# Nineteen weight slots for the experts, filled in the order of reading, and first weights loaded by rows

## The chip, the cores and the metric

The program runs on one core of a Trainium2 chip. A core has TensorE (PE, matmuls and transposes), VectorE (DVE), ScalarE (ACT), GpSimd (POOL), and SyncE (SP), which here only issues DMAs. ACT and POOL issue DMAs too; the transfers of all queues run on the same 16 DMA engines. The metric is device time in microseconds, lower is better. The kernel before takes 425.59 us, the median of three runs (425.16 to 427.43).

## The reference

One inference step of a decoder layer, for 256 prompt tokens and 32 sample tokens (8 sequences of 4), width 1024, float32:

```
h = RMSNorm(x) @ w_in                       # 1024 x 5120: q, k, v of two branches, two gates
A = stick-breaking attention (8 heads x 64); B = MoBA attention (8 heads x 64)   # sample tokens: paged caches
x = x + (sigmoid(g_A) * (A @ w_proj_sb) + sigmoid(g_B) * (B @ w_proj_moba)) @ w_out
t = RMSNorm(x)
group = top 1 of 4; experts = top 2 of the group's 4; weights w from the softmaxes
x = x + sum over the two experts of w * (silu(t @ w_gate[e]) * (t @ w_up[e])) @ w_down[e]
y = RMSNorm(x) * g_final
```

The outputs are y and the new keys and values of both branches. The 16 experts have three matrices of 1 MB each: 48 MB of weights, all read.

## The kernel before, in words

**Order.** PE's order is the order of the code. Two streams are woven by hand by `Driver` (L78): dense work, and latency-bound work that is spawned with an estimated delay. In the startup, in the routing and in the end ACT and DVE are held to the order of the code as well (`manual_schedule`); elsewhere, and on SP and POOL throughout, a scheduler with a simulated timeline orders the instructions and chooses the storage of each tile when it becomes free. A DMA on SP waits in SP's order for its storage to be free, and for the landing of an earlier DMA whose semaphore it reuses.

**Startup (L201 to L304).** x arrives in three blocks of rows (two of the prompt, one of the sample) and is turned into columns by PE (L247, six groups: three blocks by two halves of the width). DVE multiplies the turned blocks by g_mix (`mul`, L232; g_mix itself is turned by PE at L251), ACT rounds the product to a high part (`high`, L236), DVE or POOL takes the low rest (`low`, L240). The first weights, 256 columns of w_in (`raw("i2")`, L317), come in two column halves of 128 columns each. ACT rounds the first half to `h` (L263), DVE subtracts for `l` (L270), and PE multiplies high by high, high by low and low by high parts (L276), the upper rows of the weights first. The second half (`h5`, `l5`, L277) goes through `held` (L347 to L351). `square(t)` gives the sum of squares of a block on ACT; the reciprocal root reaches PE as a diagonal matrix, whose product with ones is the row `rb` (L297). Constants (a table, of which the identity comes first, and the page table) are issued on ACT's queue, L160 and L161.

**Middle.** The rest of the projection, attention, the merge, w_out. PE's order runs through without a pause of note.

**Experts (L817 to the end).** Experts are taken in pairs, pr = 0 to 7. Tokens are sorted to 64 places per expert, so that one block of 128 rows serves a pair. `up(pr)` multiplies the gathered rows, in eight steps k, by the gate and up weights of both experts; `down(pr, h)` runs a while later, in the middle of `up(pr + 1)`, after its step 3. A part of the weights is a triple (pair, kind, expert of the pair): kind 0 is the gate and up weights of steps 0 to 3, kind 1 those of steps 4 to 7, kind 2 is w_down; each is 1 MB, 8 KB per partition. `parts` (L819) lists the 48 parts in the order (pr, 0), (pr, 1), (pr, 2). `ring_slot(n)` takes the n-th slot of a ring made of four pools of 8, 5, 3 and 2 slots (`RINGS`, L75), 18 in all. The first 18 parts are loaded as the pools come to be (L850 to L900, the last ones around the store of x2, `rows_out`); `ring_loads(30)` (L1159) writes the other 30, each of which waits for a slot to be read. `xes` are three buffers for rows: one is filled by PE for pair 0 (`pick`, L980), the other two by gathers for the pairs after it (`fetch`, L970).

**End.** The results of pairs 0 to 5 go to DRAM as they come (`y_d`, L1203), and `gathered()` (L1232) brings each token its two rows back by six gathers from POOL's queue (L1239) into three slots of the ring, which DVE adds to x2 (L1246). Pairs 6 and 7 are added by matmuls with a selection matrix (`combine`, L1249). DVE's written order has the adds of the gathered rows ahead of pair 7's `h` (L1164). `final_out` multiplies by g_final (`gfb`, read into xes[0] at L1143) and stores y.

Of the kernel before, what the change touches and what calls it, by code (L numbers as in the profile page):

```python
# [7 lines left out]
F32 = mybir.dt.float32  # L8
# [4 lines left out]
ALU = mybir.AluOpType  # L13
# [4 lines left out]
D = 1024  # L18
NP_, NS = 256, 32
NT = NP_ + NS  # L20
# [53 lines left out]

RINGS = (8, 5, 3, 2)  # L75

# [45 lines left out]
def build(tc, I, O):  # L122
    nc = tc.nc
# [35 lines left out]
    nc.sync.dma_start(xs[2][0:32], I["x_sample"])  # L159
    nc.scalar.dma_start(ptb, I["page_table"][None, :].broadcast_to([128, 16]))  # L160
    nc.scalar.dma_start(blob[:, 128:], I["blob"][:, 128:])  # L161

    def cc(name):
# [37 lines left out]
    def startup():  # L201

        hold = tc.manual_schedule(engines={mybir.EngineType.Activation, mybir.EngineType.DVE})
        hold.__enter__()
        r = raw("i2", w_in[:, :, 512:768])
        dg = [at.tile([128, 128], F32, tag="t2", name=f"dg{t}", bufs=5) for t in range(3)]
        junk = at.tile([128, D], F32, tag="pg", name="junk", bufs=5)
# [33 lines left out]

        warm(2, 416)
        for i in range(6):
            ks, cols, n = place(i)
            pv = P(("at", "at", "at", "at", "ss", "po")[i], f"xt{i}")[:, 0:4 * n].rearrange("p (k t) -> p k t", k=4)
            for k in range(4):
                nc.tensor.transpose(pv[:, k, :], xsrc[i % 3][:, (ks.start + k) * 128:(ks.start + k + 1) * 128], ident[:n, :n])  # L247
            pvs.append(pv)
            if i == 0:
                pg = P("mm", "gm")  # L250
                nc.tensor.transpose(pg[:, 0:8], g8, ident[0:8, 0:8])  # L251
                V.tensor_copy(gmix, pg[:, 0:8])
        square(0)
        square(1)
        for i in range(4):
# [6 lines left out]
        h = wp.tile([128, 8, 128], F32R, tag="wh", name="hi4")  # L262
        nc.scalar.copy(h, r[:, :, 0:128])  # L263
        mul(4)
# [12 lines left out]
        h5 = split_h(r[:, :, 128:256], "i5")  # L277
        l5 = split_l(r[:, :, 128:256], h5, "i5")
        square(2)
        keep_raw(0)  # L280
# [10 lines left out]
        second = held(h5, l5, ks_of(xTh, 8), ks_of(xTl, 8), o5)  # L291
        for _ in range(6):
            next(second)
# [18 lines left out]
    def raw(key, src, shape=(8, 256)):  # L312
        if key not in raws:
            t = wr.tile([128, *shape], F32, tag="raw", name=f"raw{key}")
            if key == "i2":
                for hf in range(2):
                    nc.sync.dma_start(t[:, :, hf * 128:(hf + 1) * 128], src[:, :, hf * 128:(hf + 1) * 128])  # L317
            else:
                load = nc.sync.dma_start(t, src)
                if key in ring_after:  # L320
                    with tc.issue_after(load.ins):
                        ring_loads(ring_after[key])
            raws[key] = t
        return raws[key]
# [493 lines left out]
    W = {}  # L818
    parts = [(pr, kind, i) for pr in range(8) for kind in (0, 1, 2) for i in range(2)]  # L819

# [58 lines left out]
    V.memset(lg, 0.0)  # L879
    xes = [wk.tile([128, D + 4], F32, name=f"xe{i}") for i in range(3)]  # L880
    for i in range(3):
        nc.gpsimd.memset(xes[(i + 1) % 3], 0.0)
    nc.gpsimd.dma_start(y_d[NONE:, :], xes[0][0:16, 0:D])
# [85 lines left out]
    def fetch(pr):  # L969
        return nc.gpsimd.indirect_dma_start(out=xes[1 + pr % 2], out_offset=None, in_=x2_d[:, :],  # L970
                                            in_offset=bass.IndirectOffsetOnAxis(ap=inv[:, pr:pr + 1], axis=0),
                                            bounds_check=NT - 1, oob_is_err=False)


    def pick(c):
        po = P("at", f"xe0{c}")
        cs = slice(c * 512, c * 512 + 512)
        for t in range(3):
            mm(po, slots_of(t, 0), x2[:TW[t], t, cs], start=(t == 0), stop=(t == 2))
        (nc.scalar.copy, V.tensor_copy)[c](xes[0][:, cs], po)  # L980

# [36 lines left out]
    for t in range(3):  # L1018
        mm(pi[:, 16:17], slots_of(t, 0), x2[:TW[t], t, D:D + 1], start=(t == 0), stop=(t == 2))
    pick(0)  # L1020
    index_mm(0, 3)
# [6 lines left out]
    V.tensor_copy(rsl[0], pi[:, 16:17])  # L1028
    turn_xe(xeTs[0], xes[0], 0)
    V.tensor_reduce(es, ee, axis=AX.X, op=ALU.add)  # L1030
# [50 lines left out]
    def overflow():  # L1081
        cnt = nc.values_load(mxi[0:1, 0:1], min_val=0, max_val=NT)
        xnT = [mo.tile([128, 4, 128], F32, tag="yl", name=f"oxn{i}", bufs=2) for i in range(2)]
        wt = xes[2][:, 0:512].rearrange("p (k f) -> p k f", k=4)
        wdt = xes[2][:, 512:1024]
        hh = mo.tile([128, 256], F32, tag="h", name="ohh")
        hT = mo.tile([128, 256], F32, tag="hT", name="ohT")
        cwe = mo.tile([128, 2], F32, name="cwe")
        with tc.If(cnt > CAP):
            for t in range(3):  # L1090
                n = TW[t]
                r = x2[:n, t, D:D + 1]
                nc.scalar.dma_start(xes[1][:n], x2_d[t * 128:t * 128 + n, :])
                for k in range(8):
                    pt = P("at", f"ox{t}{k}")
                    nc.tensor.transpose(pt[:, 0:n], xes[1][:n, k:D:8], ident[:n, :n])
                    V.tensor_scalar_mul(xnT[k // 4][:, k % 4, 0:n], pt[:, 0:n], gpk[:, k:k + 1])
# [30 lines left out]

    gfb = xes[0][:, 0:D]
    fz = xes[1][:, 0:D]  # L1130

    def turn(pr):
        xeT = gt.tile([128, 4 * NT], F32, tag="xT", name=f"xeT{pr}")[:, 0:D].rearrange("p (k t) -> p k t", k=8)
        rsl[pr] = mo.tile([128, 1], F32, tag="rsl", name=f"rsl{pr}", bufs=3)
        i = turn_xe(xeT, xes[1 + pr % 2], pr)
        with tc.issue_after(i.ins):
            V.tensor_copy(rsl[pr], xes[1 + pr % 2][:, D:D + 1])  # L1137
        xeTs[pr] = xeT

    def up(pr):  # L1140
        pt = P("mm", f"gu{pr}")
        if pr == 6:
            nc.sync.dma_start(gfb, I["g_final"][None, :].broadcast_to([128, D]))  # L1143
        for k in range(8):
# [24 lines left out]
    def down(pr, h):  # L1169
# [16 lines left out]
        if LATE <= pr < 7:  # L1186
            y = mo.tile([128, D], F32, tag="y", name=f"y{pr}")
        for c in range(2):
# [85 lines left out]
    def final_square(t, c):  # L1274
        n = TW[t]
        junk = gt.tile([128, 4 * NT], F32, tag="xT", name=f"fj{t}{c}")[:, 0:512]
        nc.scalar.activation(junk[:n], x2[:n, t, c * 512:(c + 1) * 512], AF.Square, accum_out=st[:n, t, c:c + 1])
        if t == 1:
            nc.gpsimd.tensor_tensor(fz[:, c * 512:(c + 1) * 512], x2[:, t, c * 512:(c + 1) * 512], gfb[:, c * 512:(c + 1) * 512], op=ALU.mult)
        if c:  # L1280
            V.tensor_scalar(st[:n, t, 2:3], st[:n, t, 0:1], 1.0 / D, EPS, op0=ALU.mult, op1=ALU.add)
            nc.scalar.activation(st[:n, t, 3:4], st[:n, t, 1:2], AF.Ln, bias=st[:n, t, 2:3], scale=1.0 / D)
            nc.scalar.activation(st[:n, t, 3:4], st[:n, t, 3:4], AF.Exp, scale=-0.5)
# [3 lines left out]
    def final_out(t):  # L1287
# [5 lines left out]
        for u in range(2 if t < 2 else 1):  # L1293
            us = slice(u * 512, (u + 1) * 512) if t < 2 else slice(0, D)
            if t == 1:
                V.tensor_scalar_mul(fz[:, us], fz[:, us], st[:n, t, 3:4])
                nc.sync.dma_start(out[:, us], fz[:, us])
                continue
            V.scalar_tensor_tensor(y[:, us], x2[:n, t, us], st[:n, t, 3:4], gfb[:n, us], op0=ALU.mult, op1=ALU.mult)
            nc.sync.dma_start(out[:, us], y[:, us])  # L1300
# [52 lines left out]
```

## Time and profile before

| | |
|---|---|
| median of three runs | 425.59 us |
| profiled execution, its own time | 427.94 us |
| its span, first to last instruction | 426.2 us |
| PE busy | 396.5 us (93%) |
| DVE, ACT, POOL busy | 201.7, 177.5, 97.2 us |
| mean granted TensorE clock | 0.971 of full speed |
| moved by DMA | 111.65 MB, mean 262 GB/s |
| of the chain that ended last | PE 69%, DMA 21%, DVE 4% |

Rows of the order of instructions give the start in us from the span's start, the duration in us, engine, line, operation, the tile written and those read, and in brackets the engine's idle time before and what ended it; SPq is a DMA issue on SP. Rows of merged instructions carry a count. The stage table adds the granted clock and the mean busy share of the 16 DMA engines, with their rate.

### The profile page before, as it was taken

Reading aid. Unit: us, or ns where it says so; the run is one execution under the profiler, and the core shown is the slowest. Engines: PE = TensorE matmul, PEld = TensorE weight load, DVE = VectorE, ACT = ScalarE, POOL = GpSimd, SP = SyncE. Lnnn points to the kernel's source line nnn. Section 1 sums busy time; section 2 is a strip of 40 time slices with the busy share of each in tenths; the row PEclk is TensorE's granted clock in tenths of the full one; section 3 lists DMA queues with packets and bytes.
Section 4 is the critical chain, followed back from the end, with each engine's and each line's share of the span. In section 5 each row is a group of like instructions: output and inputs, shape, how many; then the busy total and the mean of one; then the engine's idle time right before and its main releaser. Section 6 shows DMA issues by size and latency. Waiting matters only on the chain.

```text
span 426.2 us, 7063 instructions
## 1 busy us (share of the span) xinstructions
PE 396.5 (93%) x2687; PEld 294.9 (69%) x2687; DVE 201.7 (47%) x424; ACT 177.5 (42%) x346; POOL 97.2 (23%) x130
## 2 busy tenths in 40 slices
PE   7899999999999999999999999998999999959491
PEld 4899989858887977988999999953433333313130
DVE  2864568467344754244657963155411111101665
ACT  5744358667562853674443552140011111101223
POOL 2750222114334313300000413411022220023011
PEclk9999999999999999999999999998999999988867
DMA  7999636637745924836899999573899999999203
GB/s 231 321 320 303 219 101 228 224 100 240 255 127 187 342 96 166 308 114 159 275 401 348 364 343 408 188 263 109 273 398 396 417 412 417 419 400 416 72 0 118
DMA packets 57960, 111.65 MB, mean 262 GB/s; under 512 B 7652, under 2 KB 37996, under 8 KB 55872
## 3 DMA queue, kind: packets, MB, share of 16 engines
q1 hardware_dynamic: 50048, 86.23, 57.0%
q0 software_dynamic: 7280, 24.47, 15.9%
q8 instruction: 23, 0.38, 0.4%
q10 hardware_dynamic: 592, 0.43, 0.3%
q14 instruction: 17, 0.14, 0.1%
HBM read 104.72 MB, written 7.96 MB: 264 GB/s over the span
## 4 chain that ended last, share of the span: by engine, by line
PE 69%; DMA 21%; DVE 4%; ACT 2%; issue 2%; POOL 1%; SPq 0%; DVEq 0%
DMA w<-in_w_expert_up 12%; PE g L347 10%; PE g L351 9%; PE g L348 9%; PE gu L1146 4%; DMA w<-in_w_expert_down 4%; DMA yg<-y_d,rows 3%; PE pk L616 3%; PE pd L1192 2%; DMA rawi<-in_w_in 2%; PE p L347 2%; PE p L351 2%; PE p L348 2%; PE ss L622 2%; PE o L347 2%
## 5 line engine op out<-in xcount | busy, mean ns | idle before, releaser
L347 PE MATMUL g<-xTh,hi 128*128 128x288 f32 x312 | 90.6, 312 | 0.0
L348 PE MATMUL g<-xTl,hi 128*128 128x288 f32 x312 | 85.7, 295 | 0.0
L1146 PE MATMUL gu<-w,xeT 128*64 128x512 f32 x256 | 64.1, 630 | 5.6 <-DMA w<-in_w_expert_up 5.2
L347 PEld LDWEIGHTS g<-xTh,hi 128*128 128x128 f32 x312 | 58.8, 188 | 0.7 <-issue 0.7
L348 PEld LDWEIGHTS g<-xTl,hi 128*128 128x128 f32 x312 | 58.8, 189 | 0.0
L351 PE MATMUL g<-xTh,li 128*128 128x288 f32 x312 | 50.0, 298 | 0.0
L333 DVE TENSOR_TENSOR li<-rawi,hi 128x1024 fp32r<-128x1024 f32 x39 | 47.3, 1214 | 2.3 <-ACT hi L328 2.3
L1146 PEld LDWEIGHTS gu<-w,xeT 128*64 128x64 f32 x256 | 19.3, 143 | 40.7 <-issue 38.4
L328 ACT CAST hi<-rawi 128x1024 fp32r<-128x1024 f32 x39 | 40.8, 1048 | 15.1 <-PE g L348 14.5
L351 PEld LDWEIGHTS g<-xTh,li 128*128 128x128 f32 x312 | 43.5, 188 | 1.7 <-issue 1.7
L1192 PE MATMUL pd<-w,hT 128*64 128x512 f32 x128 | 31.2, 632 | 0.0
L1164 DVE SCALAR_TENSOR_TENSOR h<-gu,rsl,h 128x256 f32<-128x256 f32 x8 | 3.9, 481 | 40.0 <-ACT h L1161 39.9
L617 ACT COPY KT<-pk 128x512 f32<-128x512 f32 x30 | 18.6, 639 | 7.1 <-PE pk L616 7.0
L990 DVE TENSOR_TENSOR xeT<-xe,gpk 128x512 f32<-128x512 f32 x16 | 10.4, 686 | 23.2 <-PE xe L988 23.2
L1192 PEld LDWEIGHTS pd<-w,hT 128*64 128x64 f32 x128 | 9.0, 145 | 17.4 <-issue 14.8
L970 POOL DMA_INDIRECT xe<-x_d,inv x7 | 7.3, 1037 | 55.8 <-DVE rsl L1137 26.2
L616 PE MATMUL pk<-blob,kp 128*128 128x128 f32 x128 | 19.4, 274 | 0.1
L1202 ACT COPY y<-pd 128x512 f32<-128x512 f32 x12 | 7.0, 585 | 28.3 <-PE pd L1192 28.3
L1161 ACT ACTIVATE h<-gu,rsl 128x256 f32<-128x256 f32 x8 | 3.8, 472 | 34.8 <-DVE rsl L1137 17.7
L1178 ACT COPY hT<-ph 128x256 f32<-128x256 f32 x8 | 3.0, 372 | 35.2 <-PE ph L1176 23.6
L348 PE MATMUL p<-oTl,hp 128*128 128x288 f32 x64 | 17.6, 295 | 0.0
L347 PE MATMUL p<-oTh,hp 128*128 128x288 f32 x64 | 17.5, 298 | 0.0
(301 smaller groups left out, 706.5 us busy)
## 6 DMA issues: line engine op xcount, KB each, us to landing
rawi<-in_w_in SPq DMA_DIRECT2D x19, 1024.0 KB, 5.7
w<-in_w_expert_gate SPq DMA_DIRECT2D x32, 512.0 KB, 10.1
w<-in_w_expert_up SPq DMA_DIRECT2D x32, 512.0 KB, 14.7
w<-in_w_expert_down SPq DMA_DIRECT2D x16, 1024.0 KB, 7.7
rawo<-in_w_out SPq DMA_DIRECT2D x4, 1024.0 KB
y_d<-y POOLq DMA_DIRECT2D x12, 256.0 KB, 7.6
rawp<-in_w_proj_sb SPq DMA_DIRECT2D x2, 1024.0 KB
rawp<-in_w_proj_moba SPq DMA_DIRECT2D x2, 1024.0 KB
```

The costliest lines, as they stand in the source:

```text
L328: nc.scalar.copy(h, src)
L333: V.tensor_sub(l, src, h.bitcast(F32))
L347: mm(o, h[:, k, :], mh[k], start=(k == 0), stop=False)
L348: mm(o, h[:, k, :], ml[k], start=False, stop=False)
L351: mm(o, l[:, k, :], mh[k], start=False, stop=(k == n - 1))
L616: nc.tensor.transpose(pv[:, j, :], kp[:, c, j * 128:(j + 1) * 128], ident)
L617: nc.any.tensor_copy(kt[:, :, c:256:2], pv)
L622: mm(pt[32 * bb:32 * bb + 32, 0:260], Qb[:, j, 4 * G + bb, :, :].rearrange("p h q -> p (h q)"), KT[bb][:, j, :], start=(j == 0), stop=(j = ...
L970: return nc.gpsimd.indirect_dma_start(out=xes[1 + pr % 2], out_offset=None, in_=x2_d[:, :], in_offset=bass.IndirectOffsetOnAxis(ap=inv[:, ...
L990: i = V.tensor_mul(xeT[:, ks, :], pv, gpk[:, ks, None].broadcast_to([128, 4, 128]))
L1146: mm(pt[64 * i:64 * i + 64, :], xeTs[pr][:, k, 64 * i:64 * i + 64], W[pr, k // 4, i][:, :, k % 4, :], start=(k == 0), stop=(k == 7))
L1192: mm(pd[64 * i:64 * i + 64, :], hT[:, k, 64 * i:64 * i + 64], W[pr, 2, i][:, k, c * 512:(c + 1) * 512], start=(k == 0), stop=(k == 1))
```

## The change

- `RINGS` becomes (8, 5, 3, 3), 19 slots. Room for it comes from `xes`, two buffers instead of three, and from the tile `y` of pair 6, which now takes ring slot 52. Pair 0's rows go to a tile `xe0` in the storage of the turned x; `fetch` uses xes[pr % 2].
- `parts` follows PE's reading: (0,0), (0,1), then for each pair (pr + 1, 0), (pr, 2), (pr + 1, 1), and (7, 2) last, both experts of each.
- g_final goes to ring slot 53, allocated in up(6).
- Startup: the halves of the first weights are row halves (all 256 columns of 512 rows each); the constants are issued on SP behind them; `h` is rounded in two pieces; g_mix is turned before x; square(1) goes behind l5; rb's products come two steps later in the second projection.

```diff
-RINGS = (8, 5, 3, 2)
+RINGS = (8, 5, 3, 3)
...
-    nc.scalar.dma_start(ptb, I["page_table"][None, :].broadcast_to([128, 16]))
-    nc.scalar.dma_start(blob[:, 128:], I["blob"][:, 128:])
...
         r = raw("i2", w_in[:, :, 512:768])
+        nc.sync.dma_start(blob[:, 128:], I["blob"][:, 128:])
+        nc.sync.dma_start(ptb, I["page_table"][None, :].broadcast_to([128, 16]))
...
         warm(2, 416)
+        pg = P("mm", "gm")
+        nc.tensor.transpose(pg[:, 0:8], g8, ident[0:8, 0:8])
+        V.tensor_copy(gmix, pg[:, 0:8])
         for i in range(6):
...
-            if i == 0:
-                pg = P("mm", "gm")
-                nc.tensor.transpose(pg[:, 0:8], g8, ident[0:8, 0:8])
-                V.tensor_copy(gmix, pg[:, 0:8])
         square(0)
-        square(1)
...
-        nc.scalar.copy(h, r[:, :, 0:128])
+        for a in range(2):
+            nc.scalar.copy(h[:, 4 * a:4 * a + 4, :], r[:, 4 * a:4 * a + 4, 0:128])
...
         l5 = split_l(r[:, :, 128:256], h5, "i5")
+        square(1)
         square(2)
...
-        for _ in range(6):
+        for _ in range(8):
             next(second)
...
-                    nc.sync.dma_start(t[:, :, hf * 128:(hf + 1) * 128], src[:, :, hf * 128:(hf + 1) * 128])
+                    nc.sync.dma_start(t[:, 4 * hf:4 * hf + 4, :], src[:, 4 * hf:4 * hf + 4, :])
...
-    parts = [(pr, kind, i) for pr in range(8) for kind in (0, 1, 2) for i in range(2)]
+    use = [(0, 0), (0, 1)]
+    for pr in range(7):
+        use += [(pr + 1, 0), (pr, 2), (pr + 1, 1)]
+    parts = [(*u, i) for u in use + [(7, 2)] for i in range(2)]
...
-    xes = [wk.tile([128, D + 4], F32, name=f"xe{i}") for i in range(3)]
-    for i in range(3):
-        nc.gpsimd.memset(xes[(i + 1) % 3], 0.0)
+    xes = [wk.tile([128, D + 4], F32, name=f"xe{i}") for i in range(2)]
+    for i in range(2):
+        nc.gpsimd.memset(xes[i], 0.0)
...
+    xe0 = gt.tile([128, 4 * NT], F32, tag="xT", name="xe0")
     pick(0)
...
-    gfb = xes[0][:, 0:D]
-    fz = xes[1][:, 0:D]
+    gfb = []
+    fz = xes[0][:, 0:D]
...
-            nc.sync.dma_start(gfb, I["g_final"][None, :].broadcast_to([128, D]))
+            gfb.append(ring_slot(53, "gfb")[:, 0:D])
+            nc.sync.dma_start(gfb[0], I["g_final"][None, :].broadcast_to([128, D]))
...
-            y = mo.tile([128, D], F32, tag="y", name=f"y{pr}")
+            y = ring_slot(52, f"y{pr}")[:, 0:D]
```

## Rows read from the trace of the kernel before

**Rows 1.** Chain of waits, whole program: start us, us, what.

```profile
2.14 9.07 DMA rawi<-in_w_in
...
387.76 13.81 DMA yg<-y_d,rows
```

**Rows 2.** Stage table: stretch, each engine busy (count), granted clock, DMA share, GB/s.

```profile
294.00:298.00 4.00, 4.00 (x18) 1.59 (x14) 2.38 (x7) 0.00 (x0) 0.00 (x0) 0.84 0.03 9
...
310.00:377.00 67.00, 66.81 (x320) 24.63 (x316) 9.26 (x22) 11.39 (x23) 10.85 (x16) 1.00 1.02 412
377.00:394.00 17.00, 11.95 (x40) 3.59 (x42) 2.48 (x4) 2.01 (x5) 5.91 (x6) 0.80 1.02 408
394.00:398.00 4.00, 4.00 (x20) 1.82 (x17) 3.10 (x4) 2.33 (x5) 0.00 (x0) 1.00 0.73 185
```

**Rows 3.** Order of instructions, 6 to 20 us: start, us, engine, line, tiles.

```profile
6.82 0.72 PEld L247 LDWEIGHTS xt<-blob,xs 128*128 128x128 f32 x4 [0.20 <-DMA xs<-in_x_prompt]
6.82 4.14 PE L247 MATMUL xt<-blob,xs 128*128 128x128 f32 x20
...
11.04 0.87 DVE L232 TENSOR_TENSOR xg<-xt,gmix 128x512 f32<-128x512 f32 x2
11.23 1.04 ACT L263 CAST hi<-rawi 128x1024 fp32r<-128x1024 f32 x1 [1.50 <-DMA rawi<-in_w_in]
...
12.31 1.22 DVE L270 TENSOR_TENSOR li<-rawi,hi 128x1024 fp32r<-128x1024 f32 x1 [0.40 <-ACT hi L263]
...
12.33 1.33 PE L276 MATMUL g<-xTh,hi 128*128 128x288 f32 x4 [1.38 <-ACT hi L263]
...
13.46 1.99 DVE L240 TENSOR_TENSOR xTl<-xg,xTh 128x512 fp32r<-128x512 f32 x2
...
16.45 0.69 PE L276 MATMUL g<-xTl,hi 128*128 128x288 f32 x4
...
19.56 0.40 ACT L298 COPY rb<-rb 128x288 f32<-128x288 f32 x1 [2.48 <-PE rb L297]
```

**Rows 4.** DMA queues, 6 to 8.5 us (q1 SP, q10 ACT): packets, MB, share.

```profile
q1 hardware_dynamic: 460, 0.25, 35.1%
q10 hardware_dynamic: 217, 0.30, 35.0%
```

**Rows 5.** DMA packets, 9 to 11 us: all queues together.

```profile
DMA packets 1179, 0.62 MB, mean 308 GB/s; under 512 B 20, under 2 KB 1173, under 8 KB 1179
```

**Rows 6.** Order of instructions on SP, 291 and 351 us.

```profile
291.46 0.34 SPq L1143 DMA_DIRECT2D xe<-in_g_final  x1
...
351.52 0.33 SPq L847 DMA_DIRECT2D w<-in_w_expert_gate  x1
```

**Rows 7.** Order of instructions on ACT, 365 us.

```profile
364.76 0.47 ACT L1161 ACTIVATE h<-gu,rsl 128x256 f32<-128x256 f32 x1 [2.85 <-PE gu L1146]
```

**Rows 8.** Order of instructions on PE, 373 to 397 us.

```profile
373.21 3.60 PE L1146 MATMUL gu<-w,xeT 128*64 128x512 f32 x16
380.48 1.83 PE L1146 MATMUL gu<-w,xeT 128*64 128x512 f32 x2 [3.67 <-DMA w<-in_w_expert_up]
383.88 4.52 PE L1146 MATMUL gu<-w,xeT 128*64 128x512 f32 x10 [1.57 <-DMA w<-in_w_expert_up]
...
389.68 3.60 PE L1192 MATMUL pd<-w,hT 128*64 128x512 f32 x16
393.11 3.60 PE L1146 MATMUL gu<-w,xeT 128*64 128x512 f32 x16
```

**Rows 9.** Order of instructions on all engines, 381 to 406 us.

```profile
381.23 1.06 POOL L1239 DMA_INDIRECT yg<-y_d,rows  x1 [6.38 <-issue]
...
400.75 3.78 DVE L1246 SCALAR_TENSOR_TENSOR x<-yg,w,x 128x1024 f32<-128x1024 f32 x3 [2.33 <-DMA yg<-y_d,rows]
...
405.56 0.70 PE L1176 MATMUL ph<-blob,h 128*128 128x128 f32 x2 [6.79 <-DVE x L1261]
```

**Rows 10.** DMA issues by line: KB each, median us to landing.

```profile
w<-in_w_expert_up SPq DMA_DIRECT2D x32, 512.0 KB, 14.7
```

More of the change, by code (lines that the diff above doesn't have):

```diff
@@ L969, in fetch @@
     def fetch(pr):
-        return nc.gpsimd.indirect_dma_start(out=xes[1 + pr % 2], out_offset=None, in_=x2_d[:, :],
+        return nc.gpsimd.indirect_dma_start(out=xes[pr % 2], out_offset=None, in_=x2_d[:, :],
                                             in_offset=bass.IndirectOffsetOnAxis(ap=inv[:, pr:pr + 1], axis=0),
@@ L979, in pick @@
             mm(po, slots_of(t, 0), x2[:TW[t], t, cs], start=(t == 0), stop=(t == 2))
-        (nc.scalar.copy, V.tensor_copy)[c](xes[0][:, cs], po)
+        (nc.scalar.copy, V.tensor_copy)[c](xe0[:, cs], po)
     def turn_xe(xeT, xe, pr):
@@ L1028, in build @@
     V.tensor_copy(rsl[0], pi[:, 16:17])
-    turn_xe(xeTs[0], xes[0], 0)
+    turn_xe(xeTs[0], xe0, 0)
     V.tensor_reduce(es, ee, axis=AX.X, op=ALU.add)
@@ L1083, in overflow @@
         xnT = [mo.tile([128, 4, 128], F32, tag="yl", name=f"oxn{i}", bufs=2) for i in range(2)]
-        wt = xes[2][:, 0:512].rearrange("p (k f) -> p k f", k=4)
-        wdt = xes[2][:, 512:1024]
+        wt = xes[1][:, 0:512].rearrange("p (k f) -> p k f", k=4)
+        wdt = xes[1][:, 512:1024]
         hh = mo.tile([128, 256], F32, tag="h", name="ohh")
@@ L1092, in overflow @@
                 r = x2[:n, t, D:D + 1]
-                nc.scalar.dma_start(xes[1][:n], x2_d[t * 128:t * 128 + n, :])
+                nc.scalar.dma_start(xes[0][:n], x2_d[t * 128:t * 128 + n, :])
                 for k in range(8):
                     pt = P("at", f"ox{t}{k}")
-                    nc.tensor.transpose(pt[:, 0:n], xes[1][:n, k:D:8], ident[:n, :n])
+                    nc.tensor.transpose(pt[:, 0:n], xes[0][:n, k:D:8], ident[:n, :n])
                     V.tensor_scalar_mul(xnT[k // 4][:, k % 4, 0:n], pt[:, 0:n], gpk[:, k:k + 1])
@@ L1134, in turn @@
         rsl[pr] = mo.tile([128, 1], F32, tag="rsl", name=f"rsl{pr}", bufs=3)
-        i = turn_xe(xeT, xes[1 + pr % 2], pr)
+        i = turn_xe(xeT, xes[pr % 2], pr)
         with tc.issue_after(i.ins):
-            V.tensor_copy(rsl[pr], xes[1 + pr % 2][:, D:D + 1])
+            V.tensor_copy(rsl[pr], xes[pr % 2][:, D:D + 1])
         xeTs[pr] = xeT
@@ L1278, in final_square @@
         if t == 1:
-            nc.gpsimd.tensor_tensor(fz[:, c * 512:(c + 1) * 512], x2[:, t, c * 512:(c + 1) * 512], gfb[:, c * 512:(c + 1) * 512], op=ALU.mult)
+            nc.gpsimd.tensor_tensor(fz[:, c * 512:(c + 1) * 512], x2[:, t, c * 512:(c + 1) * 512], gfb[0][:, c * 512:(c + 1) * 512], op=ALU.mult)
         if c:
@@ L1298, in final_out @@
                 continue
-            V.scalar_tensor_tensor(y[:, us], x2[:n, t, us], st[:n, t, 3:4], gfb[:n, us], op0=ALU.mult, op1=ALU.mult)
+            V.scalar_tensor_tensor(y[:, us], x2[:n, t, us], st[:n, t, 3:4], gfb[0][:n, us], op0=ALU.mult, op1=ALU.mult)
             nc.sync.dma_start(out[:, us], y[:, us])
```

## The prediction

> **What bounds the kernel now.** I read four views: the chain of waits for the ends of the program, the stage table for what each stretch is full of, then the order of instructions at the start and at the end, where the chain leaves PE. In the chain the reader is to see two long DMA pieces that PE stands behind: the first weights (2.14 to 11.21) and the gather of the expert rows that ends at 401.57 [rows 1]. Between about 20 and 290 us the chain is PE alone, so whatever PE gains at the start is carried through. The stage table then shows what the expert stage is made of [rows 2]. Ahead of 298 us the DMA engines stand nearly empty (9 GB/s); from 310 to 377 both PE (66.81 of 67 us) and the DMA engines (share 1.02, 412 GB/s) are full; from 377 to 394 the engines stay full and PE does not; from 394 on the rate falls to 185 GB/s, which is the tail of the gather. So the slots filled ahead of 298 are a lead that PE uses up, and the lead is gone at 377. The end is not set by PE, which stands idle again before its last matmuls.
>
> **The change part by part.**
>
> *Start.* PE begins the first projection at 12.33, after 1.38 us idle behind ACT's rounding of the weights, which itself waited 1.50 us for the first column half [rows 3]. The transposes that stand before it in PE's written order end at 6.82 + 4.14 = 10.96, so PE cannot start before that, whatever lands. The moved parts, each in turn:
> - The constants move from ACT's queue to SP's, behind both halves. Before, SP's weights (0.25 MB) shared the engines between 6 and 8.5 us with ACT's constants (0.30 MB, the larger part) [rows 4]. With these gone the weights get that time too. A half of 0.52 MB at the 308 GB/s that the column halves reached once alone [rows 5] takes 1.7 us; starting at about 6, the first row half is there at about 8 to 9 (an estimate), the second at about 10 to 11. Bounds: no earlier than 8; and 11.23, where the first half was before, in which case nothing is gained.
> - square(1) leaves ACT ahead of the rounding and goes behind h5. ACT has 2.48 us idle ahead of its copy of rb [rows 3], and a square with its two small followers is shorter than that. I take nothing for it. The rounding in two pieces costs one more instruction on ACT, between two instructions that wait for DVE; nothing.
> - gm goes ahead of the first transposes. The second block's transposes wait for x_prompt in any case (6.82, its weight load 0.20 us idle behind that landing [rows 3]), so the 0.3 us of gm disappear; if g_mix landed late it would cost its lateness, at most the 1.38 gained.
> - What is late next: PE reaches the low parts of columns 4 to 7 at 16.45; they were ready at 13.46 + 1.99 = 15.45. PE comes 1.38 sooner, 15.07. DVE stood idle 0.40 before li, but its own products end at 11.04 + 0.87 = 11.91, so the low parts come about 0.36 sooner, 15.09 [rows 3]. That is nearly a tie; I take off 0.08 for it, an estimate. The move of rb two steps later shifts work within PE and adds none.
> Term: 1.38 - 0.08 = 1.3 us, bounds 0 and 1.4.
>
> *The nineteenth slot.* One part is 512 KB each of an expert's gate and up weights, or its whole w_down: 1.05 MB. At the 408 to 412 GB/s of the full stretch [rows 2] that is 2.56 us, moved out of the full stretch into the empty one ahead of 298. The idle stretch has room: 4 us at 9 GB/s. If it all fell on the gather of pair 1's rows instead, it would cost up to 2.56 there; the nearest row is the empty stretch, so zero. By the Trainium skill's page DMA: Bandwidth & Descriptors, section Bandwidth, HBM feeds a core at some 358 GB/s; one slot would then be 2.93 us and the copy of g_final below 1.46, and the sum would come out 0.2 lower. This case's rows at 408 to 412 GB/s disagree, and I use them.
>
> *g_final.* Its 0.52 MB went out at 291.46, in the empty time [rows 6]. Now it takes the place of a used weight slot that comes free only after the second half of up(5) (ACT's h at 364.76 [rows 7]), so it falls into the full stretch: 1.28 us back. Nobody waits for it until POOL's product near 414. If it runs behind the gather it costs nothing, so bounds 0 and 1.28; it is issued on SP after the last weights, before the gather's packets are through, and I take 1.28.
>
> *The order of reading.* The last parts used to come as (6,2), (7,0), (7,1), (7,2). PE wanted (7,0) at 373.21 + 3.60 = 376.81 and waited 3.67 and 1.57 us for its two experts, the second until 383.88 [rows 8]. In the new order two parts fewer are ahead of it (5.1 us) and the stream is 2.56 ahead: 383.88 - 7.7 = 376.2, no wait. In its place (6,2) comes at 383.88 - 2.56 = 381.3; pd of pair 6 began at 389.68, and without the 5.24 us of waits it begins at 384.4: covered. (7,1) was read from 393.11, now from 387.9, and lands at most 2.56 sooner than before, so up to 2.7 us of wait may return. Either way PE is done 2.6 to 5.2 us sooner, and none of it counts, because PE then stands longer at the same gate.
>
> *That gate.* POOL issues the six gathers from 381.23, after the landing of pair 5's rows, and PE's work up to pair 5 had no DMA wait, so this issue time does not move. DVE waits 2.33 us for the gathers, adds until 400.75 + 3.78 = 404.53, and only then come h and the transposes of pair 7 (405.56, PE idle 6.79) [rows 9]. The gathers share the engines with the rest of the weight stream. Both ended together, so what is taken from the stream ahead comes off the gather's end: 2.56 - 1.28 = 1.28 us, bounds 0 and 2.56. The smaller memsets (two tiles instead of three), xe0 and y6 in other storage touch nothing that is waited for.
>
> Sum against the profiled execution: 426.20 - 1.3 - 1.3 = 423.6 of span; its own time is 427.94, that is 1.74 around the span, so 425.3. That execution was 2.35 above the median of the runs, 425.59; I take the difference off the median: **423.0**.
>
> **The rivals.**
> 1. The gather gets nothing. From 394 to 398 the engines moved only 185 GB/s with the gather still open [rows 2], so its end may hang on a few slow engines, where its packets take turns with SP's for as long as SP has any; g_final keeps SP's queue filled, and the end stays where it was. For: 13.81 us from the last gather's issue to its landing [rows 1]. Against: the full rate until 394. Only the start is gained: 425.6 - 1.3 = 424.3. By the Trainium skill, page DMA: Bandwidth & Descriptors, section Queues, rings and completion order, an engine goes round the queues that have work, packet by packet; by that rule this rival's time would be the one.
> 2. The gather gets the whole slot, because g_final runs behind it: 425.6 - 1.3 - 2.56 = 421.7. For: it is the last issue on SP.
> 3. The start brings nothing: h still comes at about 12.3, because the row halves land no sooner (the rounding of the low parts needs both), or because DVE's later work eats it. Against: the constants' share of 6 to 8.5. Time 424.3.
> 4. Slower: g_final blocks SP. SP issues in order; if the scheduler puts g_final ahead of the weights of (6,1), issued from 351.52 and now about 2.6 sooner, SP stands until up(5) is read (364.76) [rows 6, 7], almost 16 us. Half the loads of w_expert_up land 14.7 us or more after their issue [rows 10], so (6,1) would land at about 379, where PE reads it at 373.2: 5.6 us of wait, and everything behind it, the gather included, some 4 us late: 425.6 - 1.3 + 4 = 428. It decides only from that place on; ahead of (7,0) the block is about 4 us and the requests in flight cover it. Against: its slot comes free after those of the last weights, so it should be ordered behind them.
>
> **How the numbers follow.** Forecast 0.52, rival 1 0.17, rival 2 0.16, rival 3 0.08, rival 4 0.07. A measurement tells 0.5%, 2.1 us, from no change: faster means below 423.5. The forecast's own spread (421.9 to 424.2, from half of each term's bounds) puts 0.42 below and 0.10 above; rival 2 is faster, 1 and 3 are same, 4 is slower: 0.58, 0.35, 0.07. The range holds the forecast, 1, 2 and 3: 420.9 (rival 2 with some more at either end) to 425.2 (rival 1 with half of the start gone).
>
> **What would show it.** Right: the first L276 matmul at about 11.0 with no wait for ACT; two loads after the store of x2 instead of one; no PE wait for w_expert_up between 376 and 384; the last gather landing, counted from the end of up(0), 1.3 us sooner; g_final issued last on SP. Wrong: a gather that lands as late as before, PE gaining less than 0.5 at the start, or SP standing for PE between 345 and 365.

## The result and the profile after

The changed kernel takes 422.64 us (median of 20 runs, 419.89 to 428.18), the kernel before 426.97 us beside it (20 runs, 423.13 to 429.44). The ratio is 0.9903 [0.9874, 0.9931]: 4.1 us less (2.9 to 5.4), where the prediction's terms sum to 2.6. Its profiled execution has a span of 420.9 us and an own time of 422.70. Here and below a ratio leaves out the runs that are more than 1.5% above the fastest of their kernel, while a median has them all.

The order of instructions at the start, which answers to [rows 3] (start, us, engine, line, tiles, idle before):

```profile
7.01 2.40 PE L250 MATMUL xt<-blob,xs 128*128 128x128 f32 x20 [0.19 <-DMA xs<-in_x_prompt]
...
9.16 0.61 ACT L262 CAST hi<-rawi 128x512 fp32r<-128x512 f32 x1
...
9.83 0.79 PE L275 MATMUL g<-xTh,hi 128*128 128x288 f32 x4 [0.41 <-ACT hi L262]
...
10.23 0.88 DVE L232 TENSOR_TENSOR xg<-xt,gmix 128x512 f32<-128x512 f32 x2
...
10.36 0.62 ACT L262 CAST hi<-rawi 128x512 fp32r<-128x512 f32 x1 [0.58 <-DMA rawi<-in_w_in]
...
11.03 1.21 DVE L269 TENSOR_TENSOR li<-rawi,hi 128x1024 fp32r<-128x1024 f32 x1
...
12.16 1.97 DVE L240 TENSOR_TENSOR xTl<-xg,xTh 128x512 fp32r<-128x512 f32 x2
12.27 0.80 PE L275 MATMUL g<-xTh,hi 128*128 128x288 f32 x4 [1.06 <-ACT xTh L236]
...
14.28 0.76 PE L275 MATMUL g<-xTl,hi 128*128 128x288 f32 x4 [0.16 <-POOL pidx L287]
```

ACT no longer waits for the first weights (1.50 us before, [rows 3]), and waits 0.58 for the second half. The low parts, DVE's last work ahead of the second projection, are ready at 12.16 + 1.97 = 14.13, before at 13.46 + 1.99 = 15.45: 1.32 sooner. SP's queue has the engines to itself, against [rows 4] (DMA queues, 6 to 8.5 us: packets, MB, share):

```profile
q1 hardware_dynamic: 789, 0.80, 108.2%
```

Before, the engines were not full there, so sharing is not all of it. From 5.5 to 7 us the two queues together kept them busy for 39%, and SP's queue alone does so for 103% after the change (DMA queues, before, then after):

```profile
q1 hardware_dynamic: 110, 0.12, 26.6%
q10 hardware_dynamic: 131, 0.04, 12.8%
```

```profile
q1 hardware_dynamic: 356, 0.41, 103.4%
```

The two other profiles with the constants on ACT's queue (e2 and e9 below) have 23% and 31% there. SP also gets its two loads of the first weights out by 5.46 before and by 3.39 after (order of instructions, before, then after):

```profile
2.14 3.32 SPq L317 DMA_DIRECT2D rawi<-in_w_in  x2
```

```profile
2.13 1.26 SPq L317 DMA_DIRECT2D rawi<-in_w_in  x2
```

What held the queues while the engines stood partly idle is not shown.

The stage table, against [rows 2] (the program runs 1.9 us earlier by then):

```profile
292.00:296.00 4.00, 4.00 (x16) 1.30 (x12) 2.52 (x7) 0.00 (x0) 0.00 (x0) 0.83 0.00 0
308.00:360.00 52.00, 52.00 (x250) 19.34 (x248) 7.53 (x18) 9.25 (x18) 9.26 (x13) 1.00 1.02 413
...
375.00:388.00 13.00, 12.22 (x55) 4.99 (x51) 1.56 (x3) 2.72 (x5) 5.93 (x6) 1.00 1.02 414
388.00:396.00 8.00, 1.94 (x3) 0.79 (x3) 5.34 (x5) 2.09 (x3) 0.00 (x0) 0.77 0.59 189
```

The full stretch ends near 388, not 394, and PE is hardly idle in it (12.22 of the last 13 us busy). SP's issues show where the slot went, against [rows 6]: gate and up weights and a w_down follow the last store at 277.61, and g_final is the last issue on SP.

```profile
278.35 0.76 SPq L850 DMA_DIRECT2D w<-in_w_expert_gate  x1
279.16 0.44 SPq L850 DMA_DIRECT2D w<-in_w_expert_up  x1
279.65 15.91 SPq L850 DMA_DIRECT2D w<-in_w_expert_down  x2
...
369.62 1.60 SPq L850 DMA_DIRECT2D w<-in_w_expert_down  x2
373.38 0.33 SPq L1148 DMA_DIRECT2D gfb<-in_g_final  x1
```

All engines at the end, against [rows 8, 9]:

```profile
371.27 6.18 PE L1151 MATMUL gu<-w,xeT 128*64 128x512 f32 x28
...
380.01 1.06 POOL L1244 DMA_INDIRECT yg<-y_d,rows  x1 [7.10 <-DMA w<-in_w_expert_up]
...
391.91 1.28 DVE L1251 SCALAR_TENSOR_TENSOR x<-yg,w,x 128x1024 f32<-128x1024 f32 x1 [2.01 <-DMA yg<-y_d,rows]
...
393.78 5.09 DVE L1251 SCALAR_TENSOR_TENSOR x<-yg,w,x 128x1024 f32<-128x1024 f32 x4
...
393.92 0.80 PE L1264 MATMUL pq<-yl,PT 128*128 128x512 f32 x1 [6.70 <-DVE yl L1214]
...
399.91 0.70 PE L1181 MATMUL ph<-blob,h 128*128 128x128 f32 x2 [4.05 <-DVE x L1266]
```

PE's two waits for w_expert_up (3.67 and 1.57) are gone; PE now stands 6.70 and 4.05 us behind DVE, which stands behind the gathers. The gate is the one of before, only earlier. The chain of waits has it, against the 13.81 us of [rows 1]:

```profile
386.56 8.91 DMA yg<-y_d,rows
```

From up(0)'s first matmul (291.72 before, 289.86 after) the last gather lands at 109.85 and at 105.61: 4.2 us sooner. DVE's last add of gathered rows ends at 112.81 and at 109.01, 3.8 us sooner. After the change its last four adds run without a wait, and the last rows land (395.47) 0.8 us before DVE comes to them (396.29), so the last landing is a measure of the gate and not quite the gate itself.

### The profile page after: what moved, and what is told of

Read it like the earlier page. It is cut to its first block, busy times and chain, and to the rows that moved or that the text cites. A ratio compares the mean times of both kernels' runs of the same rounds, so it can differ in the third digit from the quotient of the medians.

```text
span 420.9 us, 7058 instructions
## 1 busy us (share of the span) xinstructions
PE 392.0 (93%) x2687; PEld 292.4 (69%) x2687; DVE 202.1 (48%) x424; ACT 177.8 (42%) x347; POOL 95.2 (23%) x129
## 4 chain that ended last, share of the span: by engine, by line
PE 69%; DMA 18%; DVE 3%; issue 3%; ACT 3%; POOL 2%; DVEq 0%; SPq 0%; POOLq 0%
DMA w<-in_w_expert_up 12%; PE g L347 10%; PE g L351 9%; PE g L348 9%; DMA w<-in_w_expert_down 4%; PE pk L616 3%; PE gu L1151 3%; PE pd L1197 2%; DMA yg<-y_d,rows 2%; PE p L347 2%; PE p L351 2%; PE p L348 2%; PE ss L622 2%; PE o L347 2%; PE pos L647 2%
## 5 line engine op out<-in xcount | busy, mean ns | idle before, releaser
L1151 PE MATMUL gu<-w,xeT 128*64 128x512 f32 x256 | 60.4, 611 | 0.3 <-DVE xeT L993 0.3
L1197 PEld LDWEIGHTS pd<-w,hT 128*64 128x64 f32 x128 | 9.1, 145 | 17.5 <-issue 14.9
L347 PE MATMUL p<-oTh,hp 128*128 128x288 f32 x64 | 17.5, 298 | 0.0
L505 DVE TENSOR_TENSOR gate<-g,rb 128x288 f32<-128x288 f32 x16 | 7.3, 456 | 21.1 <-PE g L351 21.0
```

Of the source, the lines that this page charges most:

```text
L347: mm(o, h[:, k, :], mh[k], start=(k == 0), stop=False)
L1151: mm(pt[64 * i:64 * i + 64, :], xeTs[pr][:, k, 64 * i:64 * i + 64], W[pr, k // 4, i][:, :, k % 4, :], start=(k == 0), stop=(k == 7))
L1197: mm(pd[64 * i:64 * i + 64, :], hT[:, k, 64 * i:64 * i + 64], W[pr, 2, i][:, k, c * 512:(c + 1) * 512], start=(k == 0), stop=(k == 1))
```

## The experiments

The texts name theories by letters: A is the prediction's account of the end (a slot off the gather's end, g_final back on it), D that the order of reading counts too, F that the constants on ACT's queue held the first weights back; the other letters are rivals, told by what each expects. The readings of all profiles, in us; the last column counts from the column before it.

| profile | first matmul of projection | low parts ready | up(0) | last gather lands |
|---|---|---|---|---|
| before | 12.33 | 15.45 | 291.72 | 109.85 |
| after | 9.83 | 14.13 | 289.86 | 105.61 |
| e11, the changed kernel again | 10.71 | 14.15 | 291.93 | 105.10 |
| e1, start only | 9.42 | 14.00 | 292.52 | 108.46 |
| e2, all but the start | 12.13 | 15.22 | 293.00 | 105.28 |
| e3, g_final late | 9.21 | 13.63 | 291.65 | 103.80 |
| e4, g_final twice | 10.06 | 14.30 | 291.60 | 106.11 |
| e5, list as before | 10.71 | 14.14 | 291.12 | 108.41 |
| e6, 18 slots | 9.64 | 14.15 | 292.73 | 107.79 |
| e7, late, and rounding reordered | 9.48 | 13.20 | 289.85 | 102.29 |
| e8, column halves | 9.54 | 13.78 | 290.34 | 103.38 |
| e9, constants on ACT | 11.12 | 15.73 | 296.43 | 104.85 |
| e10, before with constants on SP | 10.39 | 14.10 | 289.94 | 108.03 |
| e12, as e7 | 9.61 | 13.37 | 289.67 | 103.96 |

A landing counted from up(0) also holds some of the granted clock. In the profiles of e7 and e8 the low clock of the routing is over when up(0) begins; in the others it lasts 3.2 to 4.1 us into up(0), and with the new list the first gather is issued 89.8 to 90.3 us after up(0) began, against 88.3 and 88.5 in e8 and e7. The time from the first gather's issue to the last landing is free of this: 20.3, 18.8 and 18.7 us with the old ring (before, e1, e10), 14.7 to 15.5 with the new one (after, e2, e8, e9, e11), 13.8 in all three profiles with g_final late (e3, e7, e12), 16.3 with g_final twice (e4) and 17.5 with 18 slots (e6).

**e1_start_only.** The kernel before with the startup's part of the diff alone (all of it, here its core).

```diff
-    nc.scalar.dma_start(blob[:, 128:], I["blob"][:, 128:])
...
         r = raw("i2", w_in[:, :, 512:768])
+        nc.sync.dma_start(blob[:, 128:], I["blob"][:, 128:])
...
-        nc.scalar.copy(h, r[:, :, 0:128])
+        for a in range(2):
+            nc.scalar.copy(h[:, 4 * a:4 * a + 4, :], r[:, 4 * a:4 * a + 4, 0:128])
...
-                    nc.sync.dma_start(t[:, :, hf * 128:(hf + 1) * 128], src[:, :, hf * 128:(hf + 1) * 128])
+                    nc.sync.dma_start(t[:, 4 * hf:4 * hf + 4, :], src[:, 4 * hf:4 * hf + 4, :])
```

> The kernel before with the startup edits alone (row halves, constants behind, g_mix first, square(1) later, rb two steps later); 18 slots, old order of parts. Theory A, two separate gains, about 1.9 us at the start and the rest at the end: ratio to before 0.9955; the first matmul of up(0) at about 290 us (before 291.7, after 289.9), PE waits for w_expert_up between 375 and 384 as before (about 5 us), and the last gather lands about 110 us after that first matmul, as before. Theory B, the start's gain in the one profile is luck of the granted clock (full from 6.6 us there, from 15.4 before) and the end pays for all: ratio 1.00, first matmul of up(0) at 291 to 292.

Measured: 0.9969 [0.9936, 1.0001], 1.3 us less (none to 2.7), which the time alone does not tell from nothing. The low parts come 1.45 us sooner; the end lands at 108.46, as with the old ring.

**e2_ring_only.** The rest of the diff alone, on the kernel before with its startup.

```diff
-RINGS = (8, 5, 3, 2)
+RINGS = (8, 5, 3, 3)
...
-    parts = [(pr, kind, i) for pr in range(8) for kind in (0, 1, 2) for i in range(2)]
+    use = [(0, 0), (0, 1)]
+    for pr in range(7):
+        use += [(pr + 1, 0), (pr, 2), (pr + 1, 1)]
+    parts = [(*u, i) for u in use + [(7, 2)] for i in range(2)]
...
-            nc.sync.dma_start(gfb, I["g_final"][None, :].broadcast_to([128, D]))
+            gfb.append(ring_slot(53, "gfb")[:, 0:D])
+            nc.sync.dma_start(gfb[0], I["g_final"][None, :].broadcast_to([128, D]))
```

> The kernel before with the rest of the change alone (19 slots, order of reading, g_final in a ring slot, two row buffers); startup as before. Theory A: ratio 0.9935 (2.3 to 3 us of the 4.1), up(0) begins at about 291.7, no PE wait for w_expert_up, the last gather lands about 105.6 us after the first matmul of up(0) (before 109.9). Theory B: ratio 0.990, the whole gain.

Measured: 0.9931 [0.9884, 0.9978], 2.9 us less (0.9 to 4.9). Its startup (order of instructions) tells what held PE before:

```profile
11.03 1.04 ACT L263 CAST hi<-rawi 128x1024 fp32r<-128x1024 f32 x1 [1.52 <-DMA rawi<-in_w_in]
...
12.13 0.79 PE L276 MATMUL g<-xTh,hi 128*128 128x288 f32 x4 [3.13 <-ACT hi L263]
...
13.25 1.97 DVE L240 TENSOR_TENSOR xTl<-xg,xTh 128x512 fp32r<-128x512 f32 x2
```

PE's transposes were done at 9.0 here, and PE stood 3.13 us for ACT, as ACT did for the weights: it is the weights that held the start. The two halves of the change sum to 1.3 + 2.9 = 4.2, as the whole does (4.1), but the sum proves little: the means of all twelve runs of e2 and of the kernel before them, 424.51 and 425.80, differ by 1.3 only. What shows the gain of this half is the landing, 105.28, as early as in the changed kernel.

**e3_gfb_late.** g_final read in `gathered()` behind the adds, into a slot that the gathers leave.

```diff
-        if pr == 6:
-            gfb.append(ring_slot(53, "gfb")[:, 0:D])
-            nc.sync.dma_start(gfb[0], I["g_final"][None, :].broadcast_to([128, D]))
...
+            if t == 1:
+                gfb.append(g[1][:, 0:D])
+                nc.sync.dma_start(gfb[0], I["g_final"][None, :].broadcast_to([128, D]))
```

> The changed kernel, but g_final is loaded only after the gathered rows of the second block are added, into that block's own gather slot, so its 0.5 MB leave the full stretch. Theory A, the gather's end follows all bytes that stand before it: 1.28 us less than the changed kernel, ratio to before 0.987, last gather landing 104.3 us after the first matmul of up(0) (changed kernel 105.6). Theory C, the gather's end hangs on turns with the queue of SP and on single slow engines, and g_final behind the weights does not touch it: ratio 0.990, landing 105.6.

**e4_gfb_twice.** g_final read two times, into both halves of its slot.

```diff
+            gf = ring_slot(53, "gfb")
...
+            for i in range(2):
+                nc.sync.dma_start(gf[:, i * D:(i + 1) * D], I["g_final"][None, :].broadcast_to([128, D]))
```

> The changed kernel with the 0.5 MB of g_final loaded twice, into the two halves of its slot. Theory A: 1.28 us more than the changed kernel, ratio to before 0.993, last gather landing 106.9 us after the first matmul of up(0). Theory C: ratio 0.990, landing 105.6.

Measured: 0.9883 [0.9846, 0.9921] and 0.9947 [0.9912, 0.9983]. The chain of waits has the time from the last gather's issue to its landing; e3, then e4:

```profile
388.16 7.29 DMA yg<-y_d,rows
```

```profile
387.96 9.75 DMA yg<-y_d,rows
```

Against 8.91 one copy less is worth 1.6, one more costs 0.8; by landings -1.3 to -1.8 and +0.5 to +1.0. The forecast's 1.28 a copy lies between. In all profiles with nineteen slots and the new list the same piece is 8.2 to 8.9 us with one copy (five profiles) and 7.3 with none (three), so the difference is not that of two single executions. The times lean the same way, with overlapping intervals. So g_final is on the path though it is SP's last issue, and the end follows the bytes ahead of it.

**e5_old_order.** Nineteen slots, the list of before.

```diff
-    use = [(0, 0), (0, 1)]
...
+    parts = [(pr, kind, i) for pr in range(8) for kind in (0, 1, 2) for i in range(2)]
```

> The changed kernel with the old list of parts, (pr,0), (pr,1), (pr,2); 19 slots and everything else as changed. Theory A, the slot and not the order moves the gather's end: last gather landing 105.5 to 106 us after the first matmul of up(0), ratio to before 0.990; the waits of PE for w_expert_up at (7,0) come back in part, some 1 to 3 us, and cost nothing because PE then waits less for the gather. Theory D, the order is worth 1 us or more: landing 106.6 or later, ratio 0.993 or more.

Measured: 0.9963 [0.9924, 1.0001]; the last gather lands at 108.41, 3 us later than in the changed kernel, though the slots are nineteen. The order of instructions:

```profile
367.45 2.79 PE L1148 MATMUL gu<-w,xeT 128*64 128x512 f32 x10 [2.28 <-DMA w<-in_w_expert_up]
...
386.07 1.06 POOL L1241 DMA_INDIRECT yg<-y_d,rows  x1 [8.26 <-DMA w<-in_w_expert_down]
```

PE waits 2.28 us for (6,0) behind (5,2) on SP; down(5) starts at 81.6 from up(0) instead of 77.9, its rows are stored later, and the gathers are issued from 94.95 instead of 90.15. This is not wholly the order of before: there the scheduler had put (6,0) ahead of (5,2) of itself, and the gathers went out at 89.5. So e5 shows that the list counts, not how much of it the kernel before lost.

**e6_slots18.** The new list with 18 slots; g_final and the output tiles change slots to suit.

```diff
-RINGS = (8, 5, 3, 3)
+RINGS = (8, 5, 3, 2)
...
```

> The changed kernel with 18 slots (8, 5, 3, 2) instead of 19, the slots of g_final and of the output exchanged so that storage still comes free in time. Theory A: the stream is one part later, 2.56 us, and the gather with it: last landing 108.2 us after the first matmul of up(0), ratio to before 0.996. Theory D, the order pays and the slot does not: landing about 106, ratio 0.991.

Measured: 0.9981 [0.9944, 1.0017]; 107.79, that is 2.2 to 2.7 later than the changed kernel's 105.61 and 105.10, where a slot was put at 2.56. From the last gather's issue:

```profile
389.56 10.96 DMA yg<-y_d,rows
```

This is 2.05 us above the changed kernel's. And it is no later than with the old ring (108.03 to 109.85 in three profiles), although g_final is now in the full stretch: the order has given back what g_final takes, and some more. By time e6 is no faster than e1 (0.9969), which has the old ring and the same start, so this rests on the landings.

**e7_late_high3.** As e3, and the fourth block of x is rounded between the two pieces of h.

```diff
         for a in range(2):
             nc.scalar.copy(h[:, 4 * a:4 * a + 4, :], r[:, 4 * a:4 * a + 4, 0:128])
+            if a == 0:
+                high(3)
...
-        for i in range(3, 6):
+        for i in range(4, 6):
```

> The kernel with g_final loaded late, and in the startup ACT rounds the fourth block of x between the two pieces of the weights, where it stood 0.58 us waiting for the second row half while PE later waited 1.06 us for those blocks. Theory A: PE's second projection begins 0.4 to 0.6 us sooner than in the changed kernel (14.3 to 14.5 instead of 14.9) and the total is 0.987 of before or a little less. Rival E: DVE's low parts bind there already, nothing is gained at that place, ratio 0.988 as with g_final late alone.

Measured: 0.9863 [0.9802, 0.9924], 419.43 us (six runs). In the changed kernel PE waits until 12.27 for that rounding, which is queued on ACT behind the second half of the weights; here (order of instructions):

```profile
9.34 0.62 ACT L236 CAST xTh<-xg 128x512 fp32r<-128x512 f32 x1
...
11.47 0.80 PE L277 MATMUL g<-xTh,hi 128*128 128x288 f32 x4 [0.60 <-ACT xTh L236]
```

**e8_col_halves.** The changed kernel with column halves.

```diff
-                    nc.sync.dma_start(t[:, 4 * hf:4 * hf + 4, :], src[:, 4 * hf:4 * hf + 4, :])
+                    nc.sync.dma_start(t[:, :, hf * 128:(hf + 1) * 128], src[:, :, hf * 128:(hf + 1) * 128])
```

> The changed kernel with the first weights in column halves again (512-byte runs), the constants still behind them on SP. Theory F, the constants out of the way give the start's gain: the first matmul of the first projection at 9.8 to 10.2 us, the second projection at about 14.9, as changed. Theory G, the row halves give it: first matmul at 11 us or later.

**e9_const_act.** The changed kernel with the constants back on ACT.

```diff
+    nc.scalar.dma_start(ptb, I["page_table"][None, :].broadcast_to([128, 16]))
+    nc.scalar.dma_start(blob[:, 128:], I["blob"][:, 128:])
...
-        nc.sync.dma_start(blob[:, 128:], I["blob"][:, 128:])
-        nc.sync.dma_start(ptb, I["page_table"][None, :].broadcast_to([128, 16]))
```

> The changed kernel with the constants on ACT's queue again, ahead of the row halves as before. Theory F, the constants behind the weights give the start: the rounding of the weights waits again, first matmul of the first projection at 11 to 12 us, second projection at 16.3 to 17 (changed kernel 9.8 and 14.9). Theory H, the order of work on ACT and PE gives it (square(1) later, g_mix first): first matmul at 10 or sooner, second projection at about 15.

**e10_const_only.** The kernel before with nothing but these two lines moved, the other way.

```diff
-    nc.scalar.dma_start(ptb, I["page_table"][None, :].broadcast_to([128, 16]))
-    nc.scalar.dma_start(blob[:, 128:], I["blob"][:, 128:])
...
         r = raw("i2", w_in[:, :, 512:768])
+        nc.sync.dma_start(blob[:, 128:], I["blob"][:, 128:])
+        nc.sync.dma_start(ptb, I["page_table"][None, :].broadcast_to([128, 16]))
```

> The kernel before with one edit alone, the constants issued on SP behind the two column halves. Theory F: the rounding starts when ACT is through with square(1) and the first three blocks, at about 9.8, first matmul at about 10.9 and second projection at 15 to 15.5 (before 12.3 and 17.0). Theory H: no more than 0.5 us sooner than before.

Measured, one time each: 420.06, 426.97 and 423.81 us; the profiles tell more. With column halves the low parts are ready at 13.78, with row halves at 13.6 to 14.3: the shape of the halves shows no worth. With the constants on ACT the waits are back (e9):

```profile
10.45 0.62 ACT L262 CAST hi<-rawi 128x512 fp32r<-128x512 f32 x1 [1.49 <-DMA rawi<-in_w_in]
11.12 0.79 PE L275 MATMUL g<-xTh,hi 128*128 128x288 f32 x4 [2.15 <-ACT hi L262]
...
11.96 0.62 ACT L262 CAST hi<-rawi 128x512 fp32r<-128x512 f32 x1 [0.89 <-DMA rawi<-in_w_in]
```

The low parts come at 15.73, later than before. With the two lines alone (e10) ACT goes on without a wait, and the low parts come at 14.10, as in the whole change:

```profile
9.29 1.04 ACT L263 CAST hi<-rawi 128x1024 fp32r<-128x1024 f32 x1
...
10.39 0.79 PE L276 MATMUL g<-xTh,hi 128*128 128x288 f32 x4 [1.35 <-ACT hi L263]
```

So moving the constants is the start's whole gain; the other moves are worth some tenths at the first matmul, none at the gate. Which of the two lines does it was not tried. The gain is carried through: the first matmul of w_out begins at 242.4 to 244.2 us in the three profiles with the constants on ACT's queue (before, e2, e9) and at 239.9 to 241.9 in the eleven others, a difference that also has some of the clock of the first 17 us in it.

**e11_after_again, e12_best_again.** The changed kernel, and e7's, on one chip.

> The changed kernel once more, beside the next one on the same chip. Expected of every theory: ratio to before 0.990, second projection at 14.7 to 15.3 us, last gather landing 105 to 106 us after the first matmul of up(0), the granted clock's drop somewhere between 276 and 297 us moving single executions by 1 to 3 us.

> The kernel with g_final late and the fourth block rounded between the pieces, once more. Theory A: 1.3 to 2.3 us less than the changed kernel beside it, ratio to before 0.985 to 0.987; second projection at about 14.2, last gather of rows landing about 103 to 104 us after the first matmul of up(0) where the clock drops after it, some 1.5 sooner where it drops ahead. If neither edit pays: 0.990.

Measured: 0.9919 [0.9882, 0.9956] and 0.9866 [0.9826, 0.9906]; medians 421.71 and 420.31, before 425.53. The version of e7 beats both kernels in the medians, the changed one by 1.4 us; the two intervals overlap, so of this last step the sign rests on e3, e7 and e12 together (0.9883, 0.9863, 0.9866, against 0.9903 and 0.9919).

## Why the prediction was right, and where it was not

*The number.* 423.0 was forecast and 422.64 measured. That close a hit is luck: the kernel before took 426.97 beside it, 1.4 more than the 425.59 from which the forecast started, and the gain was 1.5 more than the forecast's sum. The two errors nearly cancel.

*Which waits bound the kernel.* Right. Both DMA pieces of the chain moved, and the rest with them.

*The start, 1.3.* Right in size: 1.32 at the low parts, and 1.3 timed (e1, none to 2.7). Of its steps, the constants on ACT's queue were the cause (e9, e10); the row halves were not needed (e8). The reason given, that they shared the engines with the weights, covers only a part: the shares of [rows 4] add up to 70%, and those from 5.5 to 7 us to 39%. "PE cannot start before that, whatever lands" (10.96) failed: the 20 transposes took 2.40 us in after's profile, 4.14 before, and PE began at 9.83. In e11 they were slow again, and there it began at 10.71. It made no difference to the sum, since PE then waited for the fourth block's rounding and for the low parts. These I had put at 15.09, nearly a tie with PE; they came at 14.1, since DVE's products moved up by 0.8 us (to 10.23 from 11.04) and `li` by 1.3.

*The slot, 2.56, and g_final, 1.28.* Right in mechanism and size: 2.2 to 2.7 (e6), and 0.5 to 1.8 for a copy (e3, e4); from the first gather's issue 2.0 to 2.8 and 0.8 to 1.7. Rivals 1 and 2 fall: the gather gained, and g_final costs it time from the last place on SP. Rival 3 falls by the low parts (e9, e10). Rival 4 did not come up: g_final went out behind the last weights.

*The order of reading: "none of it counts".* This step failed. It made the term of the end 1.28 where 2.9 was timed (e2), and 3.5 by the landings (mean of 109.85, 108.46 and 108.03 with the old ring, of 105.61, 105.10 and 105.28 with the new): -2.5 for the slot and 1.5 for g_final leave some 2.5 us for the order by landings. By time its share is uncertain: 1.9 from the 2.9 of e2, 0.3 from the means of all its runs. I had reasoned from PE alone, which does stand longer at the gate, and left out that the order also sets how early SP's stream is through. With the old ring PE waited 4.1 to 5.2 us for up weights, and SP's last weights went out 87.4 to 88.7 us after up(0) began; with 18 slots in the new order (e6) PE waited 1.23 and they went out at 83.5; in the changed kernel there is no wait, and they go out at 81.0. That PE's waits themselves make the stream late is not shown: the engines stayed full through them (share 1.02 from 377 to 394, [rows 2]). Some 95 us after up(0) the queues still held this (q0 POOL's, the gather; q1 SP's: packets, MB, share), before and then after:

```profile
q0 software_dynamic: 622, 2.15, 33.3%
q1 hardware_dynamic: 252, 1.69, 21.9%
```

```profile
q0 software_dynamic: 636, 2.21, 33.6%
q1 hardware_dynamic: 135, 0.57, 7.5%
```

The gather has the same 2.2 MB to go; SP's queue has 1.12 MB less, g_final counted, where slot and g_final explain 1.05 - 0.52 = 0.53. The other profiles say the same, at the same place: SP's queue holds 1.43 to 1.84 MB with the old ring (e1, before, e10), 0.47 to 0.63 in after, e2, e9 and e11, 1.09 with g_final twice (e4) and 1.63 with 18 slots (e6). Without its 0.52 MB of g_final e6 holds some 0.5 MB less than the old ring with as many slots: at 410 GB/s that is 1.3 us of the order's 2.5. Most of it is lead gained early: the first slots refilled now take w_down, in before's list gate and up weights, and the engines move more in that stretch (stage table, before, then after):

```profile
300.00:304.00 4.00, 4.00 (x28) 1.90 (x25) 2.75 (x13) 0.47 (x1) 0.00 (x0) 1.00 0.92 298
```

```profile
298.00:302.00 4.00, 4.00 (x28) 1.89 (x26) 2.79 (x14) 0.42 (x1) 0.00 (x0) 1.00 0.99 404
```

That is (404 - 298) x 4 us = 0.4 MB, 1 us of the full stretch. It is the list that does it: from 8 to 80 us after up(0) the engines move 391 to 395 GB/s in the four profiles with the old list, nineteen slots (e5) or eighteen, and 396 to 400 in the ten with the new one. What makes up the rest of the order's 2.5 us is not shown; nor was a run made that keeps the order and loads other weights first.

Rival 1 rested on queues taking turns, which the Trainium skill states (page DMA: Bandwidth & Descriptors, section Queues, rings and completion order). The rows neither bear the rule out nor speak against it: at the start SP's queue had 35.1% beside ACT's 35.0%, and 108.2% alone, but with both the engines were not full. Wrong was my reading that g_final would keep SP's queue busy to the gather's end; it held 0.57 MB then, and the gather had the engines sooner.

## What to carry over

When two streams share full DMA engines and one of them ends the program, count the bytes still queued when the second starts; whatever lets that stream move more before then counts, also where PE waits for the second stream in the end. Fill slots in the order in which they are read, and put constants that are needed later behind the first weights in the same queue, not beside them in another. A bound on a start that is read from one execution holds only for the clock of that execution.

## What was not expected of the hardware

The granted clock of TensorE differs between executions of the same code. At the start the 20 transposes took 2.40 us in most profiles and 4.14 in before's, whose record of a full granted clock (2.4 GHz) begins at 15.4 us, in after's at 6.6. Later there is a fall to the lower level (1.2 GHz) somewhere between 279 and 300 us, in all profiles that I read for it, where PE has short pauses in the routing. From the first matmul of w_out to up(0) 48.3 us pass in before's and in after's profile, 52.0 in e1's, 50.4 in e3's and 50.0 in e7's; nothing of the change lies in there. In e3's profile the stage table shows this (granted clock third from the end):

```profile
288.00:292.00 4.00, 3.12 (x12) 1.92 (x12) 1.69 (x4) 0.00 (x0) 0.00 (x0) 0.50 0.33 115
```

In e7's, at the same place, the clock is full:

```profile
288.00:292.00 4.00, 3.28 (x18) 2.10 (x20) 3.06 (x12) 0.00 (x0) 0.00 (x0) 1.00 0.33 101
```

This spread is as large as the change's effect, so profiles were compared from up(0) on, at the end also from the first gather's issue, and times only over many runs.
